# Hybrid gMLP and Mamba-2 layer on one core: VectorE's instructions in the W_down loop keep the order in which the program writes them

## The chip, the core and the metric

The kernel runs on one core of a Trainium2 chip. The metric is device microseconds of one execution; the time before is the median of three runs. A core has five engines with a queue each: TensorE (PE in the profile, its weight loads PEld), VectorE (DVE), ScalarE (ACT), GpSimd (POOL) and SyncE (SP), which issues most of the DMAs. Engines wait for one another by semaphores, and an engine takes the instructions of its queue one after the other.

## What is computed

One layer over x of 1024 tokens by 1024 columns, float32: a token mixer of two branches (gMLP heads and a Mamba-2 scan) and then a feed-forward block. Only the last part matters here:

```
h = rms_norm(x, norm_ffn_pre)
f = square(relu(h @ w_up))              # 1024 x 4096
x = x + rms_norm(f @ w_down, norm_ffn_post)   # w_down: 4096 x 1024
```

## The kernel before

Every float32 operand of a large product is split in two parts, the rounded value (made by a copy on ScalarE) and the rest (a subtraction on VectorE or GpSimd), and a product is three matmuls (`mm3`): high by high, high by low, low by high. The feed-forward products use Winograd's form of Strassen's scheme: seven products of half-size blocks instead of eight. W_up leaves the combinations of f that W_down needs in DRAM (`fsp`).

**The W_down loop.** The inner dimension of 4096 is cut into 8 groups of 512 rows. Groups 0 to 6 go through the seven products; the last group is multiplied plainly in the tail. The groups are taken in sets `SG`: group 0 alone, then (1, 2), (3, 4), (5, 6). Within a set the products run in the order `ORD` = 1, 5, 6, 3, 7, 2, 4, each over all groups of the set. A step is one product of one group: 24 matmuls of 512 columns, 49 steps in all. In this text s0 to s6 are the seven steps of group 0 (products 1, 5, 6, 3, 7, 2, 4), and s7 is the first one of the set (1, 2). A pair is the two steps of one product in a set of two groups.

A product accumulates in half of PSUM (four banks, tag `pd`), and there are two halves, so consecutive products alternate: s3 and s5 use the same half, as s4 and s6 do. When a product of a set is complete, `flush` empties its half into one of four accumulators in SBUF (`acc`, 128x2048): a plain copy on ScalarE the first time (products 1, 5, 6 and 4 of group 0), and otherwise an addition on VectorE, which reads PSUM. The next product but one can't start before that.

Each step needs two operands, made ahead by `preps`:
- the f operand: a load from `fsp` (`fr`), a copy on ScalarE and a subtraction on GpSimd (`f`, four buffers)
- the W operand: rows of W_down (`wr`, three large buffers that are loaded in turn by `w_load`), for products 5, 6, 7 and 4 first a subtraction of blocks on VectorE (`wt`: t1 for product 5, t2 for 6, t3 for 7, t4 for 4), then a copy on ScalarE (`whd`) and a subtraction on VectorE (`wld`).

The loop's body, for step m, is in program order:

```
floads[m + 3]()
preps[m + 2]()
... the 24 matmuls of step m ...
if g == gs[-1]:
    flush(i, ps)
```

So the program writes VectorE's work in this order: wld of s0; t1, wld of s1; t2, wld of s2; wld of s3; t3, wld of s4; wld of s5; flush of s3; t4, wld of s6; flush of s4; wld of s7; flush of s5; and so on. In a set of two groups it is: for each pair, the preparation of both steps of the next pair, then the flush of this pair. After the loop come the preparations for the last two of the four operands of the tail (`last_prep`, `wldl` in the profile), and then the tail: 16 sums of 12 matmuls each (`pl`), for each of which VectorE adds `acc`, and per token tile a chain of small operations for the norm.

**Who sets the order.** The program only states dependences. A planner at build time runs the program in a model of the chip, and each engine takes there, of the instructions whose inputs the model has ready, the one that the program wrote first. The queues that come out are fixed. The class `Engine` wraps an engine: while its `held` is true, every instruction gets an ordering edge (no semaphore) to the engine's last held instruction, so that these keep program order. TensorE is held in W_up (`pe.held`), but not in the W_down loop or the tail. VectorE is held in the prologue and, by a line further down, in the tail.

Of the kernel before, what the change touches and what calls it, by code (L numbers as in the profile page):

```python
# [56 lines left out]
def hymba_kernel(ctx, tc, x, norm_mix_pre, w_in, gm_ln_w, gm_ln_b, gm_w_s, gm_b_s,  # L57
# [24 lines left out]
    pe, act, dve, pool = [Engine(e) for e in (nc.tensor, nc.scalar, nc.vector, nc.gpsimd)]  # L82
# [1059 lines left out]
    def rows(g, h):  # L1142
        n, gi = sg_of[g]
        return raw_tile(2 * n + h)[:, 4 * gi:4 * gi + 4, :].rearrange("p (r c) n -> p r c n", r=2)

    def w_load(n, h, gs=None):
        for g in gs or SG[n]:
            for r in range(2):
                d = nc.sync.dma_start(rows(g, h)[:, r], downs[4 * g + 2 * r + h][1])
                wr_loads.append(d.ins.name)  # L1150
# [63 lines left out]
    def flush(i, ps):  # L1214
# [3 lines left out]
        else:  # L1218
            act.copy(a_, ps)
            done.add(INTO[i])  # L1220

    w_load(0, 0)
    floads[0]()
    w_load(0, 1)
# [147 lines left out]
```

## Time and profile before

| | us |
|---|---|
| median of three runs | 1070.66 (1070.23 to 1070.66) |
| the profiled execution, its own time | 1074.9 |
| its span, first to last instruction | 1073.1 |
| PE busy in the span | 1023.7 (95%) |
| DVE busy | 743.8 (69%) |
| ACT busy | 468.6 (44%) |
| POOL busy | 313.3 (29%) |

Times in the rows are microseconds from the start of the span. Neighbouring instructions of an engine overlap by some tenths of a microsecond in the records, so the cost of one in a row of them is the distance of two starts. A matmul is recorded with 0.39 us, while one starts every 0.23 us.

### The profile page before, as it was taken

The page shows a single profiled execution, that of the slowest core. Times are in us where ns is not written, and L with a number is a line of the kernel's source. Part 1 is how long each engine was busy: PE and PEld are TensorE (multiplying, and loading weights), DVE is VectorE, ACT ScalarE, POOL GpSimd, SP SyncE. Part 2 cuts the span into 40 slices and gives each one's busy share as a digit, 9 for nine tenths or more (in the row PEclk, how much of TensorE's full clock was granted, in tenths as well). Part 3 has the DMA queues.
Part 4 walks back from the last instruction along what each step waited for, and adds up shares of the span by engine and source line. Part 5 has one row for each costly group of instructions (what it writes and reads, how often), then busy time and mean ns, then how long its engine had stood idle before and what let it go on. Part 6 is the DMA issues. An engine that isn't in the chain of part 4 may idle for free. (4 is left out here: it accounts for less than half of the span.)

```text
span 1073.1 us, 13234 instructions
## 1 busy us (share of the span) xinstructions
PE 1023.7 (95%) x4735; PEld 836.4 (78%) x4735; DVE 743.8 (69%) x1265; ACT 468.6 (44%) x642; POOL 313.3 (29%) x169
## 2 busy tenths in 40 slices
PE   5989998999999999999999999999699999999996
PEld 4777776777788888888788888787588888888885
DVE  5647978366954835677477777775976777776677
ACT  5547443244343423675444444445533333333421
POOL 4454332030001002400111111112734444444533
PEclk9999898999999999999999999999989999999998
DMA  8997745475974263766756677766842552443422
GB/s 267 313 320 279 259 172 196 137 247 185 389 269 165 97 223 121 229 195 200 249 194 219 230 235 235 228 215 238 309 157 98 177 177 84 145 152 136 145 84 98
DMA packets 138857, 216.46 MB, mean 202 GB/s; under 512 B 9652, under 2 KB 72232, under 8 KB 138792
## 3 DMA queue, kind: packets, MB, share of 16 engines
q1 hardware_dynamic: 104360, 196.74, 53.1%
q10 hardware_dynamic: 34432, 18.88, 6.0%
q8 instruction: 37, 0.61, 0.2%
q14 instruction: 28, 0.23, 0.1%
HBM read 143.73 MB, written 71.86 MB: 201 GB/s over the span
## 5 line engine op out<-in xcount | busy, mean ns | idle before, releaser
L73 PE MATMUL pd<-whd,f 128*128 128x512 f32 x752 | 234.2, 392 | 7.9 <-DVE acc L73 7.9
L73 PEld LDWEIGHTS pd<-whd,f 128*128 128x128 f32 x752 | 142.3, 189 | 38.2 <-DVE acc L73 8.4
L73 POOL TENSOR_TENSOR f<-fr,f 128x1024 fp32r<-128x1024 f32 x47 | 118.5, 2524 | 147.2 <-ACT f L73 147.2
L73 PE MATMUL pd<-wld,f 128*128 128x512 f32 x376 | 147.4, 392 | 0.8 <-DVE wld L73 0.8
L73 POOL TENSOR_TENSOR wl<-ws,wh 128x1024 fp32r<-128x1024 f32 x36 | 87.7, 2440 | 191.9 <-ACT wh L73 191.7
L73 ACT CAST f<-fr 128x1024 fp32r<-128x1024 f32 x47 | 49.4, 1053 | 146.2 <-issue 132.2
L73 POOL TENSOR_TENSOR wlb<-sa,whb 128x1024 fp32r<-128x1024 f32 x16 | 38.5, 2407 | 225.1 <-ACT whb L73 213.9
L73 PEld LDWEIGHTS pd<-wld,f 128*128 128x128 f32 x376 | 71.3, 190 | 16.1 <-DVE wld L73 1.2
L73 DVE TENSOR_TENSOR wld<-wt,whd 128x1024 fp32r<-128x1024 f32 x28 | 63.5, 2267 | 26.9 <-ACT whd L73 26.9
L73 ACT ACTIVATE u<-u 128x512 f32<-128x512 f32 (+1 forms) x66 | 44.3, 672 | 61.6 <-DVE u L73 55.7
L73 ACT CAST wh<-ws 128x1024 fp32r<-128x1024 f32 x44 | 46.1, 1049 | 53.1 <-DMA ws<-in_w_in_dram 17.5
L73 DVE TENSOR_TENSOR acc<-pd,acc 128x2048 f32<-128x2048 f32 x24 | 54.9, 2287 | 14.8 <-PE pd L73 14.8
L73 DVE TENSOR_TENSOR wld<-wr,whd 128x1024 fp32r<-128x1024 f32 x21 | 47.8, 2276 | 22.8 <-ACT whd L73 22.8
L73 ACT ACT_TABLE_LOAD x30 | 38.5, 1283 | 27.9 <-DVE gg L73 8.7
L73 PE MATMUL pe<-hTh,wh 128*128 128x512 f32 x128 | 50.3, 393 | 0.0
L73 PE MATMUL pe<-hTh,wl 128*128 128x512 f32 x128 | 49.9, 390 | 0.0
L73 PE MATMUL pe<-hTl,wh 128*128 128x512 f32 x128 | 49.9, 390 | 0.0
L73 DVE TENSOR_TENSOR u<-puB,s 128x512 f32<-128x512 f32 x32 | 22.1, 692 | 31.6 <-DMA s<-early 15.8
L73 DVE TENSOR_SCALAR gg<-gg,acs 128x128 f32<-128x128 f32 x64 | 21.4, 396 | 19.9 <-DMA gg<-acd 19.9
L73 PE MATMUL pso<-wh,mixbh 128*128 128x512 f32 x64 | 28.0, 438 | 6.6 <-DVE hTl L73 5.3
L73 DVE TENSOR_TENSOR wlc<-sa,whc 128x1024 fp32r<-128x1024 f32 x16 | 29.2, 1824 | 5.6 <-ACT whc L73 5.6
L73 ACT CAST whd<-wt 128x1024 fp32r<-128x1024 f32 x28 | 29.3, 1046 | 5.7 <-DVE wt L73 2.8
(342 smaller groups left out, 2652.2 us busy)
## 6 DMA issues: line engine op xcount, KB each, us to landing
fr<-fsp SPq DMA_DIRECT2D x49, 512.0 KB, 3.8
wu<-in_w_up_dram ACTq DMA_DIRECT2D x32, 512.0 KB, 5.1
wr<-in_w_down_dram SPq DMA_DIRECT2D x32, 512.0 KB, 5.5
wd<-wh SPq DMA_DIRECT2D x28, 512.0 KB, 4.0
wd<-wl SPq DMA_DIRECT2D x28, 512.0 KB, 5.2
wh<-wd SPq DMA_DIRECT2D x28, 512.0 KB, 4.6
wl<-wd SPq DMA_DIRECT2D x28, 512.0 KB, 4.2
fsp<-c SPq DMA_DIRECT2D x42, 256.0 KB, 2.1
```

What stands on the lines that cost most here:

```text
L73: ins = fn(*a, **k)
```

## The change

One line ahead of the loop's first loads: VectorE is held from there, so that its instructions in the W_down loop get the same ordering edges as those in the tail, and loop and tail are one chain. No instruction is added or removed. The planner plans all queues anew under these edges; those of the other engines are free as before.

```diff
@@ -1219,6 +1219,7 @@
             act.copy(a_, ps)
             done.add(INTO[i])
 
+    dve.held = True
     w_load(0, 0)
     floads[0]()
     w_load(0, 1)
```

The wrapper that the line switches on:

```
def call(*a, **k):
    ins = fn(*a, **k)
    if self.held:
        if self.last is not None:
            tc.add_manual_dep(ins.ins, self.last, order, reason="order")
        self.last = ins.ins.name
    return ins
```

## Rows read from the trace of the kernel before

**Rows 1.** Windows: length, busy of PE, PEld, DVE, ACT, POOL (instructions), clock, DMA

```profile
769.70:777.85 8.15, 0.20 (x1) 0.00 (x0) 8.15 (x4) 2.09 (x2) 8.11 (x3) 0.72 0.67 231
777.85:786.05 8.20, 8.20 (x25) 6.54 (x26) 5.64 (x4) 0.00 (x0) 0.00 (x0) 0.66 0.21 66
...
813.40:835.20 21.80, 21.80 (x97) 18.05 (x97) 16.25 (x9) 8.06 (x9) 9.63 (x4) 1.00 0.27 88
```

**Rows 2.** The chain that ended last: its two long pieces

```profile
777.85 242.26 PE pd L73 x1056
1020.12 40.81 PE pl L73 x180
```

**Rows 3.** Waits of PE from 720 to the end: total, times, longest

```profile
PE pd L73 <- DVE acc L73: 7.9, 1, 7.9
PE pd L73 <- DVE wld L73: 0.8, 1, 0.8
```

**Rows 4.** Timeline of PE around the wait: start, length, operation, [idle before]

```profile
769.51 0.39 PE L73 MATMUL pd<-whd,f 128*128 128x512 f32 x1
777.85 0.79 PE L73 MATMUL pd<-whd,f 128*128 128x512 f32 x1 [7.95 <-DVE acc L73]
...
783.52 0.39 PE L73 MATMUL pd<-wld,f 128*128 128x512 f32 x1
```

**Rows 5.** Timeline of DVE in the steady part: two flushes, two pairs apart

```profile
813.43 2.29 DVE L73 TENSOR_TENSOR acc<-pd,acc 128x2048 f32<-128x2048 f32 x1 [1.01 <-PE pd L73]
...
835.20 2.29 DVE L73 TENSOR_TENSOR acc<-pd,acc 128x2048 f32<-128x2048 f32 x1 [1.01 <-PE pd L73]
```

**Rows 6.** Timeline of DVE in the first seven steps

```profile
744.43 1.22 DVE L73 TENSOR_TENSOR wt<-wr,wr 128x1024 f32<-128x1024 f32 x1
...
750.70 2.59 DVE L73 TENSOR_TENSOR wld<-wt,whd 128x1024 fp32r<-128x1024 f32 x1 [3.91 <-ACT whd L73]
...
761.10 1.21 DVE L73 TENSOR_TENSOR wld<-wr,whd 128x1024 fp32r<-128x1024 f32 x1
762.23 3.42 DVE L73 TENSOR_TENSOR wld<-wt,whd 128x1024 fp32r<-128x1024 f32 x1
...
772.24 3.36 DVE L73 TENSOR_TENSOR wt<-wr,wt 128x1024 f32<-128x1024 f32 x1
775.52 2.28 DVE L73 TENSOR_TENSOR acc<-pd,acc 128x2048 f32<-128x2048 f32 x1
```

**Rows 7.** Timeline of POOL: five subtractions for f in the same stretch

```profile
761.07 16.74 POOL L73 TENSOR_TENSOR f<-fr,f 128x1024 fp32r<-128x1024 f32 x5 [4.39 <-ACT f L73]
```

**Rows 8.** Timeline of ACT: a copy of W that waits for VectorE

```profile
758.99 1.05 ACT L73 CAST whd<-wt 128x1024 fp32r<-128x1024 f32 x1 [2.77 <-DVE wt L73]
```

**Rows 9.** Groups of DVE from 741 to 1022: xcount, busy, mean ns

```profile
L73 DVE TENSOR_TENSOR wld<-wt,whd 128x1024 fp32r<-128x1024 f32 x28 | 63.5, 2267 | 26.9 <-ACT whd L73 26.9
```

**Rows 10.** Groups of POOL from 786 to 1000

```profile
L73 POOL TENSOR_TENSOR f<-fr,f 128x1024 fp32r<-128x1024 f32 x40 | 96.2, 2406 | 127.7 <-ACT f L73 127.7
```

**Rows 11.** Timeline of DVE from the last preparation into the tail

```profile
1016.57 2.58 DVE L73 TENSOR_TENSOR wldl<-wr,whdl 128x1024 fp32r<-128x1024 f32 x1 [2.58 <-ACT whdl L73]
1020.15 2.29 DVE L73 TENSOR_TENSOR acc<-pd,acc 128x2048 f32<-128x2048 f32 x1 [1.01 <-PE pd L73]
1022.87 0.69 DVE L73 TENSOR_TENSOR acc<-pl,acc 128x512 f32<-128x512 f32 x1 [0.43 <-PE pl L73]
...
1025.59 0.69 DVE L73 TENSOR_TENSOR acc<-pl,acc 128x512 f32<-128x512 f32 x1 [1.09 <-PE pl L73]
1028.31 0.69 DVE L73 TENSOR_TENSOR acc<-pl,acc 128x512 f32<-128x512 f32 x1 [2.03 <-PE pl L73]
```

**Rows 12.** Timeline of SP's DMA issues (xcount) in the first steps

```profile
748.24 1.83 SPq L1149 DMA_DIRECT2D wr<-in_w_down_dram  x4
752.24 4.85 SPq L1174 DMA_DIRECT2D fr<-fsp  x2
```

**Rows 13.** DMA issues of the f loads: count, KB each, median us to landing

```profile
fr<-fsp SPq DMA_DIRECT2D x49, 512.0 KB, 3.8
```

## The prediction

> **What bounds the kernel now.** I read the windows by stage first, then the chain of waits, then the timelines of each engine around the place that these point to. The windows show that the W_down loop is TensorE's: in a steady stretch PE is busy without a gap at full clock, while VectorE works three quarters of the time [rows 1]. The chain that ended last is PE's from 777.85 to the end of the tail's sums [rows 2]. So time can only come from places where PE stands. From 720 on there are two: one wait of 7.9 us for an `acc`, one of 0.8 for a `wld` [rows 3].
>
> PE's timeline gives the place. The matmul at 769.51 is the last of s4; the one at 777.85 is the first of s5 [rows 4]. A step takes 5.44 us: the flushes at 813.43 and 835.20 are four steps apart, 21.77 / 4 [rows 5], so one matmul takes 5.44 / 24 = 0.227. s4 was thus over at 769.51 + 0.23 = 769.74, and PE lost 8.11 us. Behind the wait it runs slowly: 13 matmuls, from 777.85 to 783.52, take 5.67 us [rows 4] where 13 x 0.227 = 2.95 are due, 2.72 more. The clock column shows why: granted 0.72 of full in the idle window and 0.66 in the one behind it, 1.00 later [rows 1]; 0.5 would be the lower of its two levels, 1.2 GHz, and 5.67 is about twice 2.95. Wait and slow clock together are **10.8 us**, and they have one cause.
>
> The cause is in VectorE's timeline. s5 needs the half of PSUM that s3 filled. s3 ended one step ahead of s4, at 769.74 - 5.44 = 764.3, but its flush started at 775.52, 11.2 us later [rows 6]. Four instructions (two `wld`, two `wt`) stand ahead of it from 762.23, at 13.29 / 4 = 3.32 us each. The program writes all four behind this flush; the planner put them ahead, because its model had not yet finished s3. On the chip they were slow besides: alone such an operation takes 762.23 - 761.10 = 1.13 [rows 6], while next to GpSimd's subtractions (five in 16.74, 3.35 each [rows 7]) both engines seem to take turns.
>
> **The change, part by part.** Nothing is added or removed; VectorE's queue is reordered, and others are replanned.
>
> (a) The flush of s3. Program order before it: wld of s3, t3, wld of s4, wld of s5. The wld of s2 ended at 750.70 + 2.59 = 753.29 [rows 6]. From there: four operations of 1.13, and between t3 and the wld of s4 a copy of 1.05 on ScalarE [rows 8], that VectorE now has to sit out: 5.6, so it is ready for the flush at 758.9, before s3 ends. If every one of them took 3.36 [rows 6], it would be 767.8. The flush starts at 764.3 and ends at 766.6, 3.1 us before s5 wants it; in the bad case at 770.1, 0.4 late. Saved: the 10.8.
>
> (b) What is late next: the flush of s4, wanted at 769.74 + 5.44 = 775.2 by s6, stands behind t4, a copy and the wld of s6. From 766.6 that is 1.13 + 1.05 + 1.13 and 2.28 for the flush itself: 772.2, in time by 3.0. With 3.36 for both, and from the bad case's 770.1: 770.1 + 7.77 + 2.28 = 780.1, 4.9 late. Between 0 and 4.9 us; I take 0.6, near the lower end, since the bad case needs six GpSimd subtractions between 753 and 775, each met at its start.
>
> (c) Steady part. Of seven pairs, four prepare W operands that need a `wt`. In program order nothing of VectorE's can stand between `wt`, ScalarE's copy and `wld`, so such a pair costs 2 x (1.13 + 1.05 + 1.13) + 2.28 for the flush = 8.9 us of the 10.88; the other three 2 x 1.13 + 2.28 = 4.5. To this come meetings with GpSimd. The mean `wld` took 2.267 [rows 9], 1.14 above 1.13; if each `wt` met as much, pairs cost 13.5 and 6.8, 10.6 on the mean, under 10.88. In ORD at most two of the long ones follow each other, so VectorE falls back by at most 2 x 2.6 = 5.2 and recovers. A flush has a whole pair until its half is needed (5.2 + 2.28 < 10.88), and the first `wld` of a pair, at 2.6 + 2.28 + 2.27 + 1.05 + 2.27 = 10.5, is just in time. So no wait for PE: 0.
>
> A rule of the Trainium skill bears on that figure ("SBUF — State Buffer", section "Who interferes with whom"): a VectorE instruction with two SBUF inputs and a GpSimd one that reads SBUF lock each other out, and the second waits until the first is over. The trace agrees: 3.42 against 1.21 for the same operation [rows 6]. By the rule a meeting can cost a whole GpSimd operation instead of the mean 1.14; what this would make of the time is rival A.
>
> (d) The tail. Before, the four `wldl` are done (the last from 1016.57) when the last flush starts at 1020.15 [rows 11]. The program writes the third and fourth behind that flush. They now start at 1020.15 + 2.28 = 1022.4 and end at 1024.7. TensorE's first sum wants the third with its eighth matmul, 1020.12 + 7 x 0.227 = 1021.7, and the fourth with its eleventh. If PE keeps to the order of the sums it stands 1.9 and then 0.4 us: 2.3. If the planner lets it begin the next sums in the meantime (three other banks are free), 0: VectorE starts the tail's additions 1.9 us later than 1022.87, but its idle times ahead of the first additions, 0.43 + 1.09 + 2.03 [rows 11], take that up. No row shows which it will be; VectorE's own queue shows the planner filling waits with later work. I take 0.8.
>
> (e) The 0.8 us wait at s2 [rows 3] hangs on a copy and a meeting with GpSimd; t2, done early now, comes later. It stays, or is gained (the lower bound).
>
> Sum: -10.8 + 0.6 + 0 + 0.8 = **-9.4 us**, in the profiled execution (1074.9, span 1073.1). It runs 4.2 above the median, and I see no reason why the wait should differ with that: 1070.66 - 9.4 = **1061.3**. Own range: -11.6 (10.8 and 0.8) to -10.8 + 4.9 + 2.3 = -3.6, or 1059.1 to 1067.1.
>
> **Rivals.**
>
> A, slower: VectorE becomes the bound of the steady part. A pair holds two subtractions of GpSimd of 2.41 [rows 10]. If VectorE sat out both in full, pairs would cost 13.7 and 9.3, on the mean (4 x 13.7 + 3 x 9.3) / 7 = 11.8, 0.9 more than 10.88; over the 21 pairs 20 us, less some 4 of slack: 16, so -9.4 + 16 = +6.6, 1077. It decides from a mean meeting of (76.2 - 4 x 8.9 - 3 x 4.5) / 7 = 3.9 us per pair. For it: the waiting for ScalarE's copies leaves VectorE no freedom. Against it: by (c) the mean is 3.6 at most, and 2.3 if only `wld` meets.
>
> B, a wait in SyncE's queue takes the place of the one removed. Behind four `wr` loads for the set (1, 2), at 748.24, stand the f loads of s4 and s5 [rows 12]. That buffer is freed by t3, which read it at 744.43 [rows 6]; in program order t3 ends at 753.29 + 2 x 1.13 = 755.6, up to 760. If SP's order stays, the f loads go out at about 757.4 to 762 instead of 752.24; with 3.8 to land [rows 13], 1.05 for the copy and 2.41 for the subtraction, f of s4 is there at 764.7 to 769.3, while s4 starts at 764.3. Up to 5 us come back: 1066. Against it: SP's queue is planned anew, and the f loads were written ahead of those `wr` loads.
>
> C, no change: the replanned queues of ScalarE or TensorE put another wait of about this size in the first ten steps, such as a copy queued behind one that waits for t4: 1070.7.
>
> **How the numbers follow.** I give the forecast 0.66, B 0.12, A 0.13, C 0.09. A measurement of this kernel can tell about 0.2%, 2.1 us. Forecast and B are faster, but for a sliver: 0.77; C and that sliver: 0.10; A: 0.13. The range leaves out A and takes in the other three: 1059 to 1071.
>
> **What the profile after would show.** PE's wait for `acc` at s5 gone, and no window of lower clock behind it; the flush of s3 starting within a microsecond of s3's end; each `wt` followed by an idle time for `whd` and its `wld`; flushes 10.88 apart as before; two `wldl` behind the last flush, and either a short PE wait for `wldl` or sums begun out of order. Wrong would be: PE waits for `wld` in the sets of two groups (A), for `f` or `fr` at s4 to s6 (B), or any wait of over 5 us in the loop.

## The result and the profile after

| | before | after |
|---|---|---|
| median, us (4 runs each, taken together) | 1070.49 (1070.23 to 1070.66) | 1063.95 (1060.79 to 1065.82) |
| ratio | | 0.9936, 95% interval 0.9911 to 0.9961 |
| the profiled execution, its own time | 1074.9 | 1065.82 |
| its span | 1073.1 | 1064.0 |
| first W_down matmul (`pd`) in the span | 741.24 | 741.89 |
| **loop**: from there to the first matmul of the tail (`pl`) | 278.71 | 267.88 |
| **tail**: from there to the end of the span | 53.1 | 54.2 |

The change made the kernel faster by 0.64%, 6.5 us by the medians (4.2 to 9.5 by the interval) and 9.1 us between the two profiled spans. The last three lines split those 9.1 us: the loop gains 10.83, the tail gives back 1.1, and the part ahead of the loop was 0.65 longer in this execution. That part differs from one execution to the next: in the 14 profiles of this study the first `pd` matmul comes anywhere from 735.9 to 742.1, though no edit touches the program there. The slow clock goes with this scatter: ahead of the loop the granted clock was 0.50 for 10.2 to 13.7 us in the five profiles with the earliest first `pd` (735.9 to 738.1), and for 17.1 to 23.9 us in the other nine. Loop and tail repeat much better, so the experiments below are read by these two.

The windows of the kernel after, in the stretches that answer to [rows 1] (columns as there):

```profile
770.30:778.45 8.15, 8.15 (x37) 6.52 (x36) 7.24 (x4) 4.72 (x5) 6.04 (x3) 1.00 0.92 335
778.45:786.65 8.20, 8.20 (x38) 6.80 (x37) 7.08 (x5) 3.77 (x3) 3.85 (x2) 1.00 0.52 174
814.10:835.90 21.80, 21.80 (x97) 18.04 (x97) 18.71 (x9) 8.05 (x9) 9.88 (x4) 1.00 0.55 191
```

The 8 us in which PE had 0.20 us of work are full, and the clock stays at 1.00. In the steady stretch PE is as full as before, but VectorE has 18.71 us of work in 21.80 instead of 16.25, with the same nine instructions.

The chain that ended last (start, length), and the waits of PE from 715 to the end (total, times, longest):

```profile
753.99 255.95 PE pd L73 x1127
...
1012.32 39.54 PE pl L73 x173
```

```profile
PE pd L73 <- DVE wld L73: 0.8, 1, 0.8
PE pl L73 <- DVE acc L73: 0.8, 1, 0.8
```

PE's long piece now begins at s2 (753.99) instead of s5 [rows 2]: between them it never stands. The 7.9 us for `acc` [rows 3] are gone, the 0.8 at s2 has stayed, and there is a new wait of 0.8 in the tail.

VectorE's timeline after, in three stretches: the first steps [rows 6], two pairs of the steady part [rows 5], the end [rows 11]:

```profile
753.86 3.41 DVE L73 TENSOR_TENSOR wld<-wr,whd 128x1024 fp32r<-128x1024 f32 x1
757.19 1.22 DVE L73 TENSOR_TENSOR wt<-wr,wr 128x1024 f32<-128x1024 f32 x1
759.58 1.23 DVE L73 TENSOR_TENSOR wld<-wt,whd 128x1024 fp32r<-128x1024 f32 x1 [1.17 <-issue]
760.72 1.22 DVE L73 TENSOR_TENSOR wld<-wr,whd 128x1024 fp32r<-128x1024 f32 x1
765.05 2.29 DVE L73 TENSOR_TENSOR acc<-pd,acc 128x2048 f32<-128x2048 f32 x1 [3.11 <-ACT f L73]
767.26 2.77 DVE L73 TENSOR_TENSOR wt<-wr,wt 128x1024 f32<-128x1024 f32 x1
771.22 2.17 DVE L73 TENSOR_TENSOR wld<-wt,whd 128x1024 fp32r<-128x1024 f32 x1 [1.19 <-ACT whd L73]
773.31 2.28 DVE L73 TENSOR_TENSOR acc<-pd,acc 128x2048 f32<-128x2048 f32 x1
...
814.13 2.29 DVE L73 TENSOR_TENSOR acc<-pd,acc 128x2048 f32<-128x2048 f32 x1 [0.84 <-PE pd L73]
816.34 2.23 DVE L73 TENSOR_TENSOR wt<-wr,wr 128x1024 f32<-128x1024 f32 x1
819.68 1.23 DVE L73 TENSOR_TENSOR wld<-wt,whd 128x1024 fp32r<-128x1024 f32 x1 [1.12 <-ACT whd L73]
820.83 3.42 DVE L73 TENSOR_TENSOR wt<-wr,wr 128x1024 f32<-128x1024 f32 x1
825.37 1.23 DVE L73 TENSOR_TENSOR wld<-wt,whd 128x1024 fp32r<-128x1024 f32 x1 [1.11 <-ACT whd L73]
826.51 2.28 DVE L73 TENSOR_TENSOR acc<-pd,acc 128x2048 f32<-128x2048 f32 x1
828.71 6.36 DVE L73 TENSOR_TENSOR wld<-wr,whd 128x1024 fp32r<-128x1024 f32 x2
835.89 2.29 DVE L73 TENSOR_TENSOR acc<-pd,acc 128x2048 f32<-128x2048 f32 x1 [0.82 <-PE pd L73]
...
890.29 2.29 DVE L73 TENSOR_TENSOR acc<-pd,acc 128x2048 f32<-128x2048 f32 x1 [0.30 <-PE pd L73]
...
1009.97 2.29 DVE L73 TENSOR_TENSOR acc<-pd,acc 128x2048 f32<-128x2048 f32 x1 [0.83 <-PE pd L73]
1012.18 2.35 DVE L73 TENSOR_TENSOR wldl<-wr,whdl 128x1024 fp32r<-128x1024 f32 x2
```

First steps: wld of s3, t3, wld of s4, wld of s5 and then the flush of s3, exactly the program's order. VectorE is ready at 761.9 and stands 3.11 us. The profile names a copy of f on ScalarE as what ended this, but the flush does not read f. Of ScalarE it needs the copy of s2's product into the same accumulator, which ran from 762.24 to 764.10. s3 ends later, by the count of PE's matmuls at 765.0, and the flush starts then, so it waited for PE. It ends at 767.3, and s5 starts at 770.4. The flush of s4 comes after t4 and wld of s6 and ends at 775.6; s6 starts at about 775.9.

Steady part: each `wt` is followed by an idle 1.1 us, ScalarE's copy, that VectorE sits out before `wld`. From the flush at 814.13 to that at 826.51 is a long pair, from there to 835.89 a short one.

PE's timeline, the loop's first matmul, the tail's first one, and the wait in the tail:

```profile
741.89 0.39 PE L73 MATMUL pd<-whd,whf 128*128 128x512 f32 x1
...
1009.77 0.39 PE L73 MATMUL pl<-whdl,f0l 128*128 128x512 f32 x1
...
1011.13 0.39 PE L73 MATMUL pl<-whdl,f0l 128*128 128x512 f32 x1
1012.32 0.50 PE L73 MATMUL pl<-whdl,f0l 128*128 128x512 f32 x1 [0.80 <-DVE acc L73]
```

Seven matmuls of the first sum run; the eighth needs the third `wldl`, which is not there. The plan goes on with the second sum, and that stands until the last flush (1009.97 + 2.29 = 1012.26) is over. No operand of it comes from the flush, so what is left is its place in PSUM: a bank of the half that this flush empties. That is argued from the program, since the trace names no bank.

### The profile page after: what moved, and what is told of

Its sections match the earlier page's. It is cut to its first block, busy times and chain, and to the rows that moved or that the text cites. A ratio compares the mean times of both kernels' runs of the same rounds, so it can differ in the third digit from the quotient of the medians.

```text
span 1064.0 us, 13190 instructions
## 1 busy us (share of the span) xinstructions
PE 1020.5 (96%) x4735; PEld 834.0 (78%) x4735; DVE 761.0 (72%) x1265; ACT 468.5 (44%) x642; POOL 313.5 (29%) x169
## 4 chain that ended last, share of the span: by engine, by line
PE 78%; DVE 10%; DMA 5%; ACT 3%; SPq 1%; issue 1%; POOL 0%; DVEq 0%; ACTq 0%; POOLq 0%
PE pd L73 25%; PE puC L73 8%; PE puB L73 8%; PE pso L73 8%; PE pe L73 6%; PE puD L73 4%; PE pl L73 4%; PE psz L73 3%; PE psv L73 3%; DMA ws<-in_w_in_dram 2%; PE psu L73 2%; PE psB L73 2%; PE psC L73 2%; DVE v L73 1%; DVE xg L73 1%
## 5 line engine op out<-in xcount | busy, mean ns | idle before, releaser
L73 ACT CAST wh<-ws 128x1024 fp32r<-128x1024 f32 x44 | 46.1, 1047 | 53.1 <-DMA ws<-in_w_in_dram 17.7
L73 DVE TENSOR_TENSOR wld<-wt,whd 128x1024 fp32r<-128x1024 f32 x28 | 36.7, 1310 | 35.2 <-ACT whd L73 34.0
L73 DVE TENSOR_TENSOR wld<-wr,whd 128x1024 fp32r<-128x1024 f32 x21 | 60.0, 2888 | 0.7 <-ACT whd L73 0.7
L73 DVE TENSOR_TENSOR wt<-wr,wt 128x1024 f32<-128x1024 f32 x14 | 35.8, 2561 | 0.0
L73 DVE TENSOR_SCALAR gg<-gg,acs 128x128 f32<-128x128 f32 x64 | 19.1, 361 | 22.2 <-DMA gg<-acd 22.2
L73 ACT ACTIVATE f<-f 128x512 f32<-128x512 f32 x32 | 20.2, 632 | 32.0 <-DVE f L73 31.5
```

What stands on the lines that cost most here:

```text
L73: ins = fn(*a, **k)
```

## The experiments

Loop and tail are taken as in the table above, one profile each. The ratio is against the kernel before on the same chip.

| kernel | loop | tail | median (runs) | ratio, 95% interval |
|---|---|---|---|---|
| before | 278.71 | 53.1 | 1070.49 (4) | |
| after | 267.88 | 54.2 | 1063.95 (4) | 0.9936 (0.9911 to 0.9961) |
| 1 held in group 0 only | 271.67 | 53.1 | 1065.22 (6) | 0.9932 (0.9905 to 0.9959) |
| 2 held from the set (3, 4) | 278.61 | 54.3 | 1071.91 (12) | 1.0009 (0.9988 to 1.0029) |
| 3 held from s7 | 268.53 | 54.2 | 1062.99 (6) | 0.9920 (0.9896 to 0.9944) |
| 4 last preparations ahead | 267.86 | 54.5 | 1062.84 (6) | 0.9909 (0.9883 to 0.9935) |
| 5 flush of s3 later | 268.5 | 54.2 | 1062.12 (4) | 0.9913 (0.9880 to 0.9946) |
| 6 PE held too | 267.88 | 55.8 | 1066.15 (10) | 0.9952 (0.9929 to 0.9976) |
| 7 seven operations ahead of the flush | 284.41 | 54.8 | 1080.71 (5) | 1.0096 (1.0063 to 1.0130) |
| 8 the same without GpSimd | 276.14 | 54.2 | 1069.32 (10) | 0.9990 (0.9967 to 1.0012) |
| 9 released for the tail | 267.88 | 53.1 | 1062.78 (6) | 0.9916 (0.9895 to 0.9937) |
| 10 tail operands a step earlier | 267.84 | 53.7 | 1061.21 (6) | 0.9901 (0.9881 to 0.9921) |
| 11 after, 12 extra operations | 275.74 | 54.3 | 1070.37 (8) | 0.9989 (0.9969 to 1.0010) |
| 12 before, 12 extra operations | 277.53 | 53.1 | 1069.32 (8) | 1.0008 (0.9982 to 1.0034) |

**1. Held through group 0 only.**

```diff
     for m, (n, g, i) in enumerate(seq):
         gs = SG[n]
+        if m == 7:
+            dve.held = False
```

> VectorE is held only until s6's flush is written, and free again in the sets of two groups; the tail's preparations are then planned freely too. Theory (the gain is the flush of s3 alone): the stretch from the first W_down matmul to the first matmul of the tail takes 267.9 us as in the changed kernel (before: 278.7), and the tail, from there to the end, 53.2 as before (changed kernel: 54.2). So about 1 us faster than the changed kernel in the profile, a span near 1063. Rival (the order through the whole loop is what pays): the loop stays between 270 and 279.

The loop took 271.67: 7.0 of the 10.8 us are gained, so the expectation that holding seven steps would do fell. The tail is that of before, as expected. VectorE's timeline of this kernel:

```profile
758.06 2.35 DVE L73 TENSOR_TENSOR wt<-wr 128x1024 f32<-128x1024 f32 x2
...
764.81 3.41 DVE L73 TENSOR_TENSOR wt<-wr,wt 128x1024 f32<-128x1024 f32 x1
768.15 2.28 DVE L73 TENSOR_TENSOR acc<-pd,acc 128x2048 f32<-128x2048 f32 x1
```

The operations written behind the release are free, and the planner puts `wt` of the next set into the held stretch, ahead of the flushes. The flush of s3 starts at 768.15 instead of with s3's end, and PE waits three times for `acc`, 0.36, 1.02 and 1.74 us. The clock stays at 1.00. So a hold must last as long as there are later operations that are ready early.

**2. and 3. Held from the set (3, 4), and held from s7 on** (each on the kernel before):

```diff
     for m, (n, g, i) in enumerate(seq):
         gs = SG[n]
+        if m == 21:
+            dve.held = True
```

```diff
     for m, (n, g, i) in enumerate(seq):
         gs = SG[n]
+        if m == 7:
+            dve.held = True
```

> VectorE is held only from the first step of the set (3, 4) on; group 0 and the set (1, 2) are planned as before. Theory: the wait of 7.9 us at s5 and the slow clock behind it stay, the loop takes 278.7, the tail 54.2: 1 us slower than before, about 1071.5. Rival (keeping the order pays or costs in the steady part): the loop differs from 278.7 by more than 1; if VectorE became the bound there, PE waits for wld or acc appear after 850.

> VectorE is held from s7 on, not in group 0. The queue then has only two operations of later steps (the wld of s6 and of s7) between the wld of s5 and the flush of s3, where before had four. Theory (what counts is how much stands ahead of that flush): at 3.3 us each beside GpSimd the flush starts at 762.2 + 6.7 = 769 and ends at 771.2, s5 waits 1.5 us (0.5 to 3), the loop takes 268.5 to 272. Rival (group 0 itself has to be held): the wait stays near 8 and the loop near 278.7.

Held from the set (3, 4), PE's wait of 7.9 us and the slow clock are all there, the loop is that of before, and the tail costs its 1.1. So the order in the steady part is worth nothing either way, and nothing that the line does in the later sets carries the gain. Held from s7, only two `wld` can come ahead of the flush of s3. VectorE's timeline of this third kernel:

```profile
765.58 3.33 DVE L73 TENSOR_TENSOR wld<-wr,whd 128x1024 fp32r<-128x1024 f32 x1 [2.38 <-ACT whd L73]
768.84 2.28 DVE L73 TENSOR_TENSOR acc<-pd,acc 128x2048 f32<-128x2048 f32 x1
```

The flush is over at 771.1 and PE waits 0.37 us, a little less than the theory asked for. The loop is 0.65 above that of after. Holding from s7 on is thus almost enough: between the `wld` of s5 and the flush it lets in the `wld` of s6 and of s7, and of the three `wt` of the next set that experiment 1 lets in ahead of the flush it lets in one, which comes early (754.11).

**4. The tail's last preparations ahead of step 48's matmuls:**

```diff
         preps[m + 2]()
+        if m == len(seq) - 1:
+            preps[m + 3]()
+            floads[m + 4]()
+            preps[m + 4]()
...
-    for m in range(len(seq) + 2, len(preps)):
-        if m + 1 < len(preps):
-            floads[m + 1]()
-        preps[m]()
```

> The changed kernel with the third and fourth preparation of the tail written ahead of the last step's matmuls and so ahead of the last flush. Theory (the tail's extra 1.1 us is the two operations behind the last flush and what they make of the order of the sums): the loop takes 267.9, the tail 53.2, the PE wait of 0.8 us for acc in the tail is gone, 1 us less than the changed kernel. Rival (the tail is longer for another reason): it stays at 54.2.

The tail did not come back to 53.1. VectorE's timeline of this kernel:

```profile
999.51 7.65 DVE L73 TENSOR_TENSOR wldl<-wr,whdl 128x1024 fp32r<-128x1024 f32 x4
1007.09 2.28 DVE L73 TENSOR_TENSOR acc<-pd,acc 128x2048 f32<-128x2048 f32 x1
```

PE began the tail at 1005.48, so the last flush could have started then; four `wldl` in 7.65 us put it 1.6 us late. PE, which now has all operands, runs the whole first sum and stands 1.06 us for `acc` ahead of the second. The second sum starts at 1009.42, when the flush (1007.09 + 2.28 = 1009.37) is over, though every operand was there. The loss of the tail is therefore the time of the last flush as much as that of the last operands.

**5. The flush of s3 written one step later** (behind the preparation of s6, all held):

```diff
         preps[m + 2]()
+        if m == 4:
+            flush(3, banks[3])
...
-        if g == gs[-1]:
+        if g == gs[-1] and m != 3:
             flush(i, ps)
```

> The changed kernel with one displacement: the flush of s3 is written behind t4 and the wld of s6. Theory: t4, ScalarE's copy and the wld take 3.3 to 7.8 us from s3's end or from where VectorE is free, so the flush ends 2 to 5 us after s4 does less the 5.4 of s4: s5 waits 0 to 3 us, and the loop takes 268 to 272. It also tells what a wait of a few us does to the clock: if the granted clock falls only after the long wait, the matmuls behind this one run at 0.227 us each; rival: any wait of over 1 us is followed by slow matmuls (0.43 us each), and the loss is larger than the wait by 1 us or more.

PE waits 0.5 us for `acc`, the clock stays at 1.00, the loop is 268.5. A short delay of this flush costs itself and no more.

**6. TensorE held as well:**

```diff
-    dve.held = True
+    dve.held = pe.held = True
```

> The changed kernel with TensorE held as well from the loop on; every other queue stays the same. Theory (in the tail TensorE was filled with later sums while wldl was late): now it waits 1.9 and 0.4 us for wldl in the first sum, the loop stays at 267.9 and the tail grows from 54.2 to 55 to 56. Rival (the order of the sums is worth nothing, since VectorE's additions start no earlier): the tail stays at 54.2 or shrinks.

The waits of PE in this kernel (the line for the tail):

```profile
PE pl L73 <- DVE wldl L73: 2.1, 2, 1.9
```

The loop is unchanged to the hundredth, and the tail takes 55.8. These are the two stands that the prediction worked out for sums in order: the first is its 1.9, the second 0.2 instead of 0.4. So the planner's filling saves 1.6 of the 2.7 us that this order costs the tail.

**7. Seven operations of later steps written ahead of the flush of s3** (t1 twice, t4 and wld of s6, t2 twice, wld of s7; the expectation says six), all held, so that the flush stands late again:

```diff
-        elif k == 5 * len(gs) + 1:
+        elif k == 5 * len(gs) + 1 and n:
             w_load(n + 1, 1)
-        floads[m + 3]()
-        preps[m + 2]()
+        if m == 3:
+            w_load(1, 1)
+        if m != 4 and m != 5:
+            floads[m + 3]()
+            preps[m + 2]()
...
+        if m == 3:
+            w_block(1, "t1")
+            w_block(2, "t1")
+            floads[7]()
+            preps[6]()
+            w_block(1, "t2")
+            floads[8]()
+            preps[7]()
+            w_block(2, "t2")
         if g == gs[-1]:
             flush(i, ps)
```

> VectorE held as in the changed kernel, but the program writes six operations of later steps (t1 twice, t4 and wld of s6, t2, wld of s7, t2) ahead of the flush of s3, about the queue that the planner had made before. Theory (the place of that flush is the whole cause): the wait at s5 and the slow clock are back, wait 6 to 10 us, loop 276 to 281. Rival (the gain comes from other queues that the planner made differently under the held order): the loop stays under 271.

VectorE's timeline and two windows of this kernel:

```profile
758.53 6.77 DVE L73 TENSOR_TENSOR wt<-wr 128x1024 f32<-128x1024 f32 x2
765.22 3.40 DVE L73 TENSOR_TENSOR wt<-wr,wt 128x1024 f32<-128x1024 f32 x1
...
778.65 4.48 DVE L73 TENSOR_TENSOR acc<-pd,acc 128x2048 f32<-128x2048 f32 x2
```

```profile
769.30:786.40 17.10, 5.42 (x13) 4.26 (x14) 13.33 (x6) 5.14 (x6) 5.97 (x2) 0.50 0.66 246
786.40:790.00 3.60, 3.60 (x18) 2.95 (x17) 0.75 (x1) 0.94 (x1) 0.00 (x0) 1.00 0.00 0
```

The flush starts at 778.65 and PE waits 13.92 us for it, more than expected: here all seven stand behind the `wld` of s5, while the planner's queue of before had three of them among the earlier `wld`, where there was time. Wait and slow clock are both back: 284.41 - 267.88 = 16.5, of which 13.9 is the wait, and 2.7 is half of the 5.42 us of matmuls that ran at a granted 0.50, since they would have taken half as long at 1.00. A held queue with the flush in the wrong place is thus worse than the planner's: it is the place that counts, not the hold.

**8. The same, with no GpSimd work in the stretch.** For s4 to s8 the low parts of f are left out; ScalarE copies the value a second time instead of GpSimd's subtraction.

```diff
-        split(*hl, fr)
+        if 4 <= len(pcs) < 9:
+            act.copy(hl[0], fr)
+            act.copy(hl[1], fr)
+        else:
+            split(*hl, fr)
```

> As the kernel with the six operations ahead of the flush, but the low parts of five f operands (s4 to s8) are a copy on ScalarE instead of a subtraction on GpSimd, so GpSimd reads nothing in that stretch (the low parts are left out of the result there). Theory (each of these VectorE operations was slow because GpSimd read SBUF at the same time): they take 1.2 us each instead of up to 3.4, the wait at s5 shrinks to 0 to 3 us, loop 268 to 273. Rival (they are slow for another reason, such as waiting for ScalarE's copies): the wait stays above 5.

VectorE's timeline and one window of this kernel:

```profile
755.83 2.35 DVE L73 TENSOR_TENSOR wt<-wr 128x1024 f32<-128x1024 f32 x2
758.10 1.22 DVE L73 TENSOR_TENSOR wt<-wr,wt 128x1024 f32<-128x1024 f32 x1
762.91 1.23 DVE L73 TENSOR_TENSOR wld<-wt,whd 128x1024 fp32r<-128x1024 f32 x1 [3.59 <-issue]
```

```profile
768.80:775.60 6.80, 5.80 (x14) 4.56 (x15) 3.14 (x2) 0.65 (x1) 0.00 (x0) 0.50 0.40 143
```

Three operations that took 6.77 and 3.40 us take 2.35 and 1.22: it was GpSimd's subtractions that made them slow (the run takes away their reading and their writing together, and does not part the two). The time did not come back in full, though. ScalarE has five copies more, VectorE sits out 3.59 us for its own copy behind them, and PE still waits 4.04 us for `acc` and 1.11 for a flush on ScalarE. With 5.80 / 2 = 2.9 of slow clock that is 8.05 of the 8.26 that the loop is above after's. The measured loop lies between the theories' sizes, and the run answers the question of the operations, not that of the wait.

**9. and 10. For the tail: VectorE released from step 45, or the tail's operands written one step earlier.**

```diff
+        if m == 45:
+            dve.held = False
```

```diff
-        floads[m + 3]()
-        preps[m + 2]()
+        if m < 46:
+            floads[m + 3]()
+            preps[m + 2]()
+        else:
+            for j in {46: (48, 49), 47: (50, 51), 48: (52,)}[m]:
+                if j + 1 < len(preps):
+                    floads[j + 1]()
+                preps[j]()
...
-    for m in range(len(seq) + 2, len(preps)):
-        if m + 1 < len(preps):
-            floads[m + 1]()
-        preps[m]()
```

> The changed kernel, but VectorE is free again for the last four steps, so that the planner can put all four wldl and the work before them ahead of the last flush. Theory (the tail's extra 1.1 us is PE reaching the second sum, whose bank the last flush must free, before that flush is over, because the first sum can't be completed without the late wldl): the loop takes 267.9, the tail 53.1 as before, no PE wait for acc after the loop; 1.1 us less than the changed kernel. Rival (VectorE falls behind in the last steps, as with all four wldl ahead of the last flush under the held order): the tail stays at 54.2 to 54.5.

> The changed kernel with the tail's four preparations written one step earlier (two in each of the last steps but one), still held: one wldl stands ahead of the last flush but one, three between the two flushes. Theory: three of them take 3 x 1.13 plus at most two meetings with GpSimd of 2.4, 3.4 to 8.2 us of the 10.9 less 2.2 that VectorE has there, so the last flush starts at once when the last product ends; loop 267.9, tail 53.1 to 53.5. Rival (a meeting with GpSimd delays the last flush again): PE waits about 1 us for acc, tail 54.2 to 54.5.

Released from step 45, the loop stays 267.88, the tail is that of before, and PE has no wait there. This is the best sum of loop and tail, 321.0 against 322.1 after and 331.8 before. Written a step earlier, the tail takes 53.7, with a wait of 0.2 for `acc`, between what theory and rival had asked for. The second has the lowest median, 1061.21, and both beat the kernel before; that they beat the kernel after is seen in the profiles' tails, but the intervals of the ratios overlap.

**11. and 12. Does the steady part have slack?** t1, t2 and t3 of groups 3 to 6 are computed twice, 12 operations more, in the kernel after and in the kernel before:

```diff
             sub(dve, t_, a_, b_)
+            if g > 2 and key != "t4":
+                sub(dve, t_, a_, b_)
```

> The changed kernel with 12 more operations on VectorE: the subtractions t1, t2 and t3 of the groups 3 to 6 are done twice (same result). Theory (held order uses up VectorE's slack in the sets of two groups: in the changed kernel's trace it waits for PE only 2.0 us in 76 us of a set): each costs 1.13 to 3.4 us, 14 to 40 in the two sets, less 4 of slack and some 5 that VectorE may fall behind; PE waits 5 to 30 us in all, the loop grows from 267.9 to 273 to 298. Rival (VectorE is busy only 72% of the time, so there is room): the loop grows by less than 2.

> The kernel before with the same 12 additional operations on VectorE, in the groups 3 to 6, where the planner is free. Theory (a free order has other operations to put where VectorE would wait for ScalarE's copies): VectorE's waits for copies in the trace of before, 2.85 us each, take them up; the loop stays within 3 of 278.7. Rival (12 operations cost the same in either order): the loop grows by as much as in the held kernel.

The waits of PE in the loop and a window of the kernel after with the extra work:

```profile
PE pd L73 <- DVE wld L73: 3.1, 4, 0.8
PE pd L73 <- ACT whd L73: 2.3, 3, 1.1
```

```profile
878.50:881.90 3.40, 3.40 (x8) 2.72 (x9) 3.37 (x2) 0.00 (x0) 2.09 (x1) 0.50 0.08 11
```

Held, the loop loses 7.9 us: PE waits six times more, for `wld` and for `whd`, and behind two of these waits the clock falls for 3.4 us. The added waits are 4.6 us and the slow clock costs 1.7; the remaining 1.6 us are not broken down here. In the order of before the same 12 operations cost nothing: PE's only waits are its old ones, 7.9 and 0.7. The loop is even shorter, 277.53 against 278.71, since the slow clock lasted 6.8 us in that profile and not 10.2: PE had 3.09 us of work in it instead of 5.61, and half of the difference is 1.3. So the held order spends slack that the free order has.

## Why the prediction was right, point by point

**(a) The flush of s3: right.** Forecast -10.8, measured -10.83 in the loop. The flush starts as s3 ends; experiments 2, 3 and 7 show that its place makes the wait and that the slow clock comes with the wait. VectorE was ready at 761.9, between the two bounds of 758.9 and 767.8, since one of the four operations between, the `wld` at 753.86, took 3.41. That the size came out to 0.03 is luck in part: the wait is the same 7.9 us in before, experiment 2 and experiment 12, but the slow clock behind it lasted 10.2, 10.2 and 6.8 us, which alone moves the loop of before by 1.2. That meetings with GpSimd are what stretches 1.2 to 3.4 us was an argument from two rows; experiment 8 shows it for GpSimd's subtractions as a whole (3.40 us beside them, 1.22 without). This agrees with the rule of the Trainium skill that the prediction named ("SBUF — State Buffer", "Who interferes with whom").

**(b) The flush of s4: taken at 0.6, measured 0.** It ended at 775.6 with about 0.3 us to spare, within the forecast's 772.2 to 780.1; s3 ended 0.7 later in this profile than in that of before. t4 and wld of s6 each met GpSimd in part (2.77 and 2.17). That it is in time was not safe: with experiment 1's order PE waits there.

**(c) The steady part: no wait, as forecast, but the parts of the sum were wrong, and it is near its edge.** From the flush at 814.13 to that at 890.29, seven pairs, are 76.16 us, of which VectorE waited 0.82 + 0.82 + 0.30 for PE. That leaves 74.2 / 7 = 10.6 us for a pair, the forecast's figure. The meetings make (74.2 - 4 x 8.9 - 3 x 4.5) / 7 = 3.6 us per pair, the upper bound of the prediction and just under the 3.9 at which rival A decides. That the mean is the forecast's is luck, since the meetings lie elsewhere than assumed. The groups from 741 to 1022 show it (columns as in [rows 9]), first two of the kernel before, then three of the kernel after:

```profile
L73 DVE TENSOR_TENSOR wld<-wr,whd 128x1024 fp32r<-128x1024 f32 x20 | 46.6, 2329 | 22.8 <-ACT whd L73 22.8
L73 DVE TENSOR_TENSOR wt<-wr,wt 128x1024 f32<-128x1024 f32 x14 | 21.5, 1534 | 0.4
```

```profile
L73 DVE TENSOR_TENSOR wld<-wr,whd 128x1024 fp32r<-128x1024 f32 x20 | 58.8, 2971 | 0.0
...
L73 DVE TENSOR_TENSOR wld<-wt,whd 128x1024 fp32r<-128x1024 f32 x28 | 36.7, 1310 | 35.2 <-ACT whd L73 34.0 <-issue 1.2
L73 DVE TENSOR_TENSOR wt<-wr,wt 128x1024 f32<-128x1024 f32 x14 | 35.8, 2561 | 0.0
```

`wld<-wt` hardly meets GpSimd any more (1310 ns instead of 2267), `wt` and `wld<-wr` do. A long pair costs 12.4 (one of the four 11.4) and not 13.5, a short one 8.6 and not 6.8, and the two errors cancel in the mean. VectorE's added work in the windows is these meetings, not new operations: its 76 `wt` and `wld` of the loop take 166.6 us together, and took 148.7 before. The prediction also expected flushes 10.88 us apart as before; most come 12.4 and 9.4 apart, behind a long pair and a short one, so that PE's pace shows only in the 21.76 us of two pairs. Experiment 11 shows how little is left.

**(d) The tail: the size nearly right (0.8 taken, 1.1 measured), a reason wrong.** The prediction said that PE could begin the next sums in three other free banks. The plan does go on with the second sum, but that sum cannot start before the last flush is over, and experiment 4 shows the same wait with all operands there; so the place that the second sum takes in PSUM was not free (that it is a bank of the flushed half is argued, as above). The upper bound of 2.3 is what experiment 6 shows as waits (2.1, the tail 2.7 longer), the lower one of 0 what experiment 9 shows.

**(e) The 0.8 us at s2** stayed, in every kernel here.

**The sum:** -10.83 + 1.1 = -9.7 in loop and tail, forecast -9.4. The medians differ by only 6.5, so the forecast of the time was 2.6 us too low; 1061.3 / 1070.66 = 0.9913 lies in the interval of the ratio, at its end. Of the rest up to 1.2 can be the slow clock of before (see (a)), which was long in the profiled execution. That what is left is the scatter of the part ahead of the loop is argued from the 735.9 to 742.1 above, and fits with the lower ratios of kernels with nearly the same loop and tail (3, 4, 5), but no run isolates it.

**The rivals.** A (VectorE the bound) did not come, by 0.3 us per pair. B (SyncE's queue) did not: SP's issues after, answering to [rows 12], are

```profile
745.77 10.80 SPq L1174 DMA_DIRECT2D fr<-fsp  x4
758.43 1.79 SPq L1149 DMA_DIRECT2D wr<-in_w_down_dram  x4
```

The plan moved the `wr` loads that wait for t3 behind the f loads, the objection that the prediction had raised. C (another wait in the first ten steps) did not: PE's only wait there is that at s2.

## What to carry to other kernels

When a bound engine stands once, look at what the engine that it waits for did in the microseconds before: here four ready but not urgent operations ahead of one urgent flush cost 10.8 us, and it was the planner that had put them there. Fix an engine's order where a late instruction holds up the bound engine, and let it go where the order costs more than it saves (experiment 9); a hold that ends too early lets later work slip in ahead (experiment 1). A fixed order makes an engine sit out every hand-over to another engine, so add these to its work per step first: the kernel after has 0.3 us per pair left, and experiment 11 loses 7.9 us to work that the free order hides (experiment 12).

## What the runs showed of the hardware that was not expected

- PE's stands carry a second price, and it does not follow from the length of the stand alone. The granted clock went to 0.50 while PE still stood in the long waits: for 6.8 us with a wait of 4.04 us (experiment 8), for 17.1 with one of 13.92 (experiment 7), and with the same 7.9 us for 10.2 in before and experiment 2, but for 6.8 in experiment 12. Single waits of up to 1.74 us (experiment 1) left it at 1.00. But two short waits, of 1.07 and 0.77 us, whose ends are 1.3 us apart, were followed by 3.4 us at 0.50 (experiment 11). The cost is half of PE's busy time in that window, 1.5 to 2.9 us here.
- Where VectorE's operations of two SBUF inputs run beside GpSimd's subtractions, 1.22 us becomes up to 3.43. The fixed order did not make the meetings fewer: it moved them to other instructions, and VectorE's 76 operations took 17.9 us more.
